# A 3x3 convolution: from a tile-scheduled, fully unrolled program to one hand-synchronised program per engine with a TensorE loop

## The chip, the cores and the metric

The kernel runs on one core of one Trainium2 chip. The metric is the time of one execution on the device in microseconds (us). The kernel before takes 125.95 us, the median of three runs (125.91 to 125.97).

## The reference

A 3x3 convolution with padding 1 and no bias: 16 images of 64 channels and 64x64 pixels, 128 output channels, all in fp32. Nine tenths of the weights are zero, at random places, and the kernel makes no use of that.

```python
x_pad = np.pad(x, ((0, 0), (0, 0), (1, 1), (1, 1)))
for b in range(16):
    for co in range(128):
        for ci in range(64):
            for kh in range(3):
                for kw in range(3):
                    output[b, co] += weight[co, ci, kh, kw] * x_pad[b, ci, kh:kh+64, kw:kw+64]
```

## The kernel before, in words

**Tiling.** Two images form a pair: 64 channels of the one on partitions 0 to 63, those of the other on 64 to 127. There are eight pairs, and each is cut into four blocks of 16 output rows, 32 blocks in all. A matmul uses 64 of the 128 rows of TensorE, so the two images of a pair go through the two halves of the array side by side; each matmul has up to 512 columns (8 rows of 64 pixels) and writes one bank of PSUM.

**Two forms of a block.** Block 0 is "direct" (`direct`, L159): for each of two groups of 8 rows, nine taps for each image, so 2 x 9 x 2 = 36 matmuls. All others use a sum shared by neighbouring rows (`twos`, L166): GpSimd adds rows pairwise into a tile `s` (L169), TensorE makes the shared product of `s` with the middle row of taps (3 taps x 2 images = 6 matmuls), ScalarE copies it from PSUM to `pc` (L176), then TensorE makes the products of the even and of the odd rows with difference weights (12 matmuls each), and VectorE adds `pc` and writes the output tile `o` (L183, four instructions a block). That is 30 matmuls a block. All matmuls stand on L150, in `product`; each is issued as a weight load and a matmul.

**Start.** SyncE (SP) loads the weights (L60) and the first 32 rows of pair 0 in fp32 (L62). GpSimd loads the rest of pair 0 (L63) and then pairs 1, 2, 3 and the first 24 rows of pair 4 (L68), converting fp32 to bf16 in the DMA. TensorE runs matmuls on zeros (`keep_busy`, L86) until the weights are there, transposes them (L111), runs seven more, and starts on block 0 when VectorE has converted the first rows (L101).

**Order.** The order of each engine's instructions is the order in which they are written; the tile framework adds the semaphores. There are eight tiles for the input, so a load never waits for a free tile. The later loads stand behind a block's GpSimd addition: the rest of pair 4 behind that of block 7, pair 5 behind block 11, pair 6 behind 15, the halves of pair 7 behind 19 and 23 (L74, L196 to L199). There are three tiles for the output, of 4 MB each. SP stores a pair when its four blocks are in the output tile (L207), and the last pair in two halves of 2 MB (L205). After the second store SP issues five loads of 4 bytes (L211), which move on which of the framework's DMA semaphores the later stores go.

Of the kernel before, what the change touches and what calls it, by code (L numbers as in the profile page):

```python
# [7 lines left out]

FP32 = mybir.dt.float32
BF16 = mybir.dt.bfloat16  # L10
ADD = mybir.AluOpType.add
SUB = mybir.AluOpType.subtract

BLOCKS = {p: "TTTT" for p in range(8)}
BLOCKS[0] = "DTTT"  # L20


G0, G1, G2, G21, G01 = range(5)
KW_ORDER = (1, 0, 2)


@with_exitstack
def kernel(
    ctx: ExitStack,
    tc: tile.TileContext,  # L30
    x: bass.AP,
    weight: bass.AP,
    out: bass.AP,
):
    nc = tc.nc

    B, C_IN, H, W = x.shape
    C_OUT, _, KH, KW = weight.shape
    assert (B, C_IN, H, W) == (16, 64, 64, 64) and (C_OUT, KH, KW) == (128, 3, 3)
    NP = B // 2  # L40
    HEAD = 32

    const_pool = ctx.enter_context(tc.tile_pool(name="const", bufs=1))
    x_pool = ctx.enter_context(tc.tile_pool(name="x", bufs=1))
    s_pool = ctx.enter_context(tc.tile_pool(name="s", bufs=3))
    p_pool = ctx.enter_context(tc.tile_pool(name="pc", bufs=4))
    o_pool = ctx.enter_context(tc.tile_pool(name="o", bufs=3))
    psum_pool = ctx.enter_context(
        tc.tile_pool(name="psum", bufs=8, space=bass.MemoryType.PSUM)
    )  # L50

    ctx.enter_context(tc.manual_schedule())


    def pair(p):
        return x[2 * p : 2 * p + 2].rearrange("n i h w -> (n i) h w")

    xs = [x_pool.tile([128, H, W], BF16, name=f"x{p}") for p in range(NP)]
    w_sb = const_pool.tile([C_OUT, C_IN * KH * KW], FP32, name="w_sb")
    nc.sync.dma_start(out=w_sb, in_=weight.rearrange("o i kh kw -> o (i kh kw)"))  # L60
    x_head = const_pool.tile([128, HEAD, W], FP32, name="x_head")
    nc.sync.dma_start(out=x_head, in_=pair(0)[:, 0:HEAD, :])  # L62
    nc.gpsimd.dma_start(out=xs[0][:, HEAD:H, :], in_=pair(0)[:, HEAD:H, :])  # L63
    ident = const_pool.tile([128, 128], BF16, name="ident")
    make_identity(nc, ident)

    def load(p, a=0, b=H):
        nc.gpsimd.dma_start(out=xs[p][:, a:b, :], in_=pair(p)[:, a:b, :])  # L68

    EARLY, CUT = 4, 24

    LATER = {2: (5,), 3: (6,), 4: (7, 0, 32), 5: (7, 32, 64)}  # L74
    for p in range(1, EARLY):
        load(p)
    load(EARLY, 0, CUT)


    idle_rhs = const_pool.tile([128, 512], BF16, name="idle_rhs")  # L80
    nc.vector.memset(idle_rhs, 0.0)  # L81
    idle_ps = psum_pool.tile([128, 512], FP32, name="ps")

    def keep_busy(n):
        for _ in range(n):
            nc.tensor.matmul(idle_ps, idle_rhs[:, 0:128], idle_rhs, start=True, stop=True)  # L86

    keep_busy(7)

    w_v = w_sb.rearrange("o (i k) -> o k i", k=KH * KW)
    w_bf = const_pool.tile([C_OUT, 3, 4 * C_IN], BF16, name="w_bf")
    w_bf4 = w_bf.rearrange("o g (k i) -> o g k i", k=4)
    wT = const_pool.tile([128, 5, 3, C_OUT], BF16, name="wT")

    def tap(g, kw, n):
        return wT[64 * n : 64 * n + 64, g, (kw - n) % 3, :]

    def cast_x(copy, a, b):  # L100
        copy(out=xs[0][:, a:b, :], in_=x_head[:, a:b, :])  # L101

    def cast(g, copy, a, b):
        k = 3 * g + a % 3
        copy(out=w_bf4[:, g, a:b, :], in_=w_v[:, k : k + b - a, :])  # L105

    def transposed(g):
        wps = psum_pool.tile([128, 4, 128], FP32, name="ps")
        for j in range(3):
            src = w_bf[:, g, C_IN * j : C_IN * (j + 2)]  # L110
            nc.tensor.matmul(wps[:, j, :], src, ident, start=True, stop=True)  # L111
        return wps[:, 0:3, :]

    def difference(g, wps):
        nc.vector.tensor_tensor(out=wT[:, g], in0=wps, in1=wT[:, G1], op=SUB)  # L115

    cast(G1, nc.vector.tensor_copy, 0, 3)
    cast(G1, nc.scalar.copy, 3, 4)
    cast(G0, nc.vector.tensor_copy, 0, 3)
    cast(G0, nc.vector.tensor_copy, 3, 4)  # L120
    cast(G2, nc.scalar.copy, 0, 3)
    cast(G2, nc.vector.tensor_copy, 3, 4)
    cast_x(nc.vector.tensor_copy, 0, 9)
    nc.scalar.copy(out=wT[:, G1], in_=transposed(G1))
    ps0 = transposed(G0)
    nc.vector.tensor_copy(out=wT[:, G0], in_=ps0)  # L126
    ps2 = transposed(G2)
    nc.scalar.copy(out=wT[:, G2], in_=ps2)
    keep_busy(7)
    cast_x(nc.scalar.copy, 9, 18)  # L130
    difference(G01, ps0)
    difference(G21, ps2)
    cast_x(nc.scalar.copy, 18, HEAD)


    def product(terms, rows):


        ps = [psum_pool.tile([128, rows, W], FP32, name="ps") for _ in range(2)]
        todo = [(t, kw) for t in terms for kw in KW_ORDER]  # L140
        for i, ((src, g, first, step), kw) in enumerate(todo):
            n_src = src.shape[1]
            lo = 0 if first >= 0 else 1
            hi = rows if first + (rows - 1) * step < n_src else rows - 1
            c_lo, c_hi = max(0, 1 - kw), min(W, W + 1 - kw)
            a = first + lo * step
            b = first + (hi - 1) * step + 1
            for n in range(2):
                q = slice(64 * n, 64 * n + 64)
                nc.tensor.matmul(  # L150
                    ps[n][:, lo:hi, c_lo:c_hi],
                    tap(g, kw, n),
                    src[q, a:b:step, c_lo + kw - 1 : c_hi + kw - 1],
                    start=(i == 0),
                    stop=(i == len(todo) - 1),
                )
        return ps

    def direct(p, o, r0, rows):  # L159
        ps = product(  # L160
            [(xs[p], G1, r0, 1), (xs[p], G0, r0 - 1, 1), (xs[p], G2, r0 + 1, 1)], rows
        )
        nc.scalar.copy(out=o[0][:, r0 : r0 + rows, :], in_=ps[0])  # L163
        nc.vector.tensor_copy(out=o[1][:, r0 : r0 + rows, :], in_=ps[1])  # L164

    def twos(p, o, r0):  # L166
        t0 = r0 // 2
        s = s_pool.tile([128, 8, W], BF16, name="s")
        nc.gpsimd.tensor_tensor(  # L169
            out=s, in0=xs[p][:, r0 : r0 + 16 : 2, :], in1=xs[p][:, r0 + 1 : r0 + 16 : 2, :], op=ADD  # L170
        )
        shared = product([(s, G1, 0, 1)], 8)
        pc = []
        for n in range(2):
            c = p_pool.tile([128, 8, W], FP32, name="pc")
            nc.scalar.copy(out=c, in_=shared[n])  # L176
            pc.append(c)
        even = [(xs[p], G21, r0 + 1, 2), (xs[p], G0, r0 - 1, 2)]
        odd = [(xs[p], G01, r0, 2), (xs[p], G2, r0 + 2, 2)]
        for first, terms in ((r0, even), (r0 + 1, odd)):  # L180
            ps = product(terms, 8)
            for n in range(2):
                nc.vector.tensor_tensor(  # L183
                    out=o[n][:, first : r0 + 16 : 2, :], in0=ps[n], in1=pc[n], op=ADD
                )

    for p in range(NP):
        both = o_pool.tile([C_OUT, 2, H, W], FP32, name="o")
        o = [both[:, n] for n in range(2)]
        into = out[2 * p : 2 * p + 2].rearrange("n o h w -> o n h w")  # L190
        last = p == NP - 1
        for blk in range(4):
            r0 = 16 * blk
            if BLOCKS[p][blk] == "T":
                twos(p, o, r0)
                if p == 1 and blk == 3:  # L196
                    load(EARLY, CUT, H)
                elif blk == 3 and p in LATER:
                    load(*LATER[p])  # L199
            else:  # L200
                for r, rows in ((r0, 8), (r0 + 8, 8)):
                    direct(p, o, r, rows)
            if last and blk % 2 == 1:
                rows = slice(r0 - 16, r0 + 16)
                nc.sync.dma_start(out=into[:, :, rows, :], in_=both[:, :, rows, :])  # L205
        if not last:
            nc.sync.dma_start(out=into, in_=both)  # L207
        if p == 1:
            spare = const_pool.tile([1, 5], FP32, name="spare")
            for k in range(5):  # L210
                nc.sync.dma_start(out=spare[:, k : k + 1], in_=weight[0:1, 0, 0, 0:1])  # L211


# [28 lines left out]
```

## Time and profile before

| what | value |
|---|---|
| median of three timed runs | 125.95 us (125.91 to 125.97) |
| span of the profiled execution | 124.3 us |
| time of a run that lies outside the span, by these two | about 1.6 us |
| TensorE busy (PE) | 108.7 us, 87% of the span, 989 matmuls |
| VectorE busy (DVE) | 82.5 us, 66% |
| ScalarE (ACT), GpSimd (POOL) | 39.0 us, 41.7 us |
| bytes written by the DMA | 42.91 MB |
| HBM read and written | 17.07 MB and 33.55 MB, 407 GB/s over the span |

The profile is of one execution, and no time was taken of that execution apart from its span. One part of the page divides the span into 40 slices and gives each engine's busy share of a slice as a digit in tenths; PEclk is the clock granted to TensorE in the same way, and DMA the busy share of the core's 16 DMA engines. Another part lists the DMA queues. A query can give the same numbers for any stretch of the span, list the instructions of a source line, and tell what each engine waited for. An `x` before a number is a count. GB/s counts bytes written at the destination; a load that converts fp32 to bf16 reads twice what it writes.

### The profile page before, as it was taken

The numbers are of one execution on the slowest core, as the hardware profiler recorded it, in microseconds if no ns is written. First come the engines' busy times: TensorE is split into PE (matmuls) and PEld (weight loads), VectorE is DVE, ScalarE is ACT, GpSimd is POOL, SyncE is SP. The second block draws the span as 40 slices with busy tenths as digits, with TensorE's granted clock in tenths as the row PEclk, the third lists the DMA queues.
The fourth block names the chain that finished last, engine by engine and source line by source line (L and its number), as shares of the span: only waits on it lengthen the run. The fifth ranks groups of instructions, "written<-read, shape, count | busy, mean of one in ns | idle before, by whom it ended". The sixth has DMA issues, their size and how long they took to land.

```text
span 124.3 us, 2453 instructions
## 1 busy us (share of the span) xinstructions
PE 108.7 (87%) x989; PEld 57.2 (46%) x989; DVE 82.5 (66%) x135; ACT 39.0 (31%) x71; POOL 41.7 (34%) x47
## 2 busy tenths in 40 slices
PE   6959999999999999999999999999999999970000
PEld 2425555555555555555555555555555555530000
DVE  0353577877787778777877878887877787772000
ACT  4543333333333333333333333333333333330000
POOL 6409333533353335333443335333333320000000
PEclk9999999999999999999999999999999999997555
DMA  4999999999999999999999999999999999999991
GB/s 120 348 220 227 219 213 213 238 411 338 335 392 422 319 316 324 377 340 329 303 385 378 354 380 443 376 349 389 418 422 437 422 427 427 437 427 403 432 414 82
DMA packets 4198, 42.91 MB, mean 345 GB/s; under 512 B 347, under 2 KB 347, under 8 KB 1115
## 3 DMA queue, kind: packets, MB, share of 16 engines
q1 hardware_dynamic: 2746, 34.90, 67.2%
q0 software_dynamic: 1440, 7.86, 30.7%
q8 instruction: 7, 0.11, 0.3%
q14 instruction: 5, 0.03, 0.1%
HBM read 17.07 MB, written 33.55 MB: 407 GB/s over the span
## 4 chain that ended last, share of the span: by engine, by line
PE 82%; DMA 5%; DVE 1%; issue 1%; DVEq 0%; SPq 0%
PE ps L150 82%; DMA x_head<-in_x_dram 5%; DVE o L183 1%; DVEq L237 0%; DVE x L101 0%; SPq L60 0%; DVEq L183 0%
## 5 line engine op out<-in xcount | busy, mean ns | idle before, releaser
L183 DVE TENSOR_TENSOR o<-ps,pc 128x512 f32<-128x512 f32 x124 | 77.8, 686 | 22.1 <-PE ps L150 19.2
L150 PE MATMUL ps<-x,wT 64*128 64x504 bf16 (+3 forms) x780 | 88.8, 373 | 1.3 <-DVE x L101 1.3
L150 PEld LDWEIGHTS <-wT 64*128 64x128 bf16 x966 | 55.2, 94 | 49.5 <-issue 1.7
L169 POOL TENSOR_TENSOR s<-x 128x512 bf16<-128x512 bf16 x31 | 35.6, 1150 | 57.6 <-PE ps L150 41.1
L176 ACT COPY pc<-ps 128x512 f32<-128x512 f32 x62 | 33.3, 589 | 64.0 <-issue 61.8
L150 PE MATMUL ps<-s,wT 64*128 64x512 bf16 (+1 forms) x186 | 25.7, 377 | 0.0
L86 PE MATMUL ps<-idle_rhs 128*128 128x512 bf16 x14 | 4.8, 505 | 1.2 <-DVE idle_rhs L81 1.2
L68 POOL DMA_DIRECT2D x<-in_x_dram x9 | 5.0, 560 | 0.0
L86 PEld LDWEIGHTS <-idle_rhs 128*128 128x128 bf16 x14 | 1.5, 118 | 3.2 <-issue 1.4
L105 DVE CAST w_bf<-w_sb 128x192 bf16<-128x192 f32 (+1 forms) x4 | 1.1, 351 | 2.5 <-DMA w_sb<-in_weight_dram 2.5
L164 DVE COPY o<-ps 128x512 f32<-128x512 f32 x2 | 1.4, 692 | 2.0 <-PE ps L150 2.0
L101 DVE CAST x<-x_head 128x576 bf16<-128x576 f32 x1 | 0.5, 460 | 2.6 <-DMA x_head<-in_x_dram 2.6
L101 ACT CAST x<-x_head 128x576 bf16<-128x576 f32 (+1 forms) x2 | 1.5, 802 | 1.8 <-DMA x_head<-in_x_dram 1.8
L163 ACT COPY o<-ps 128x512 f32<-128x512 f32 x2 | 1.2, 586 | 2.4 <-PE ps L150 2.4
L105 ACT ACT_TABLE_LOAD x1 | 1.3, 1283 | 0.7 <-PEq L226 0.7
L105 ACT CAST w_bf<-w_sb 128x64 bf16<-128x64 f32 (+1 forms) x2 | 0.7, 416 | 1.6 <-DMA w_sb<-in_weight_dram 1.6
L115 DVE TENSOR_TENSOR wT<-ps,wT 128x384 bf16<-128x384 f32 x2 | 1.0, 548 | 0.0
L111 PEld LDWEIGHTS <-w_bf 128*128 128x128 bf16 x9 | 0.5, 97 | 1.0 <-DVE w_bf L105 1.0
L63 POOL DMA_DIRECT2D x<-in_x_dram x1 | 0.7, 693 | 0.8 <-POOLq L226 0.8
L111 PE MATMUL ps<-ident,w_bf 128*128 128x128 bf16 x9 | 0.9, 222 | 0.1
L81 DVE MEMSET idle_rhs<- 128x256 uint32 x1 | 0.3, 272 | 0.9 <-PEq L226 0.9
L126 DVE CAST wT<-ps 128x384 bf16<-128x384 f32 x1 | 0.6, 551 | 0.0
(8 smaller groups left out, 1.9 us busy)
## 6 DMA issues: line engine op xcount, KB each, us to landing
out_dram<-o SPq DMA_DIRECT2D x7, 4096.0 KB, 19.8
x<-in_x_dram POOLq DMA_DIRECT2D x5, 1024.0 KB, 16.8
out_dram<-o SPq DMA_DIRECT2D x2, 2048.0 KB
x<-in_x_dram POOLq DMA_DIRECT2D x3, 512.0 KB, 13.8
x_head<-in_x_dram SPq DMA_DIRECT2D x1, 1024.0 KB, 6.2
x<-in_x_dram POOLq DMA_DIRECT2D x1, 640.0 KB, 14.8
x<-in_x_dram POOLq DMA_DIRECT2D x1, 384.0 KB, 22.3
w_sb<-in_weight_dram SPq DMA_DIRECT2D x1, 288.0 KB
```

What stands on the lines that cost most here:

```text
L68: nc.gpsimd.dma_start(out=xs[p][:, a:b, :], in_=pair(p)[:, a:b, :])
L86: nc.tensor.matmul(idle_ps, idle_rhs[:, 0:128], idle_rhs, start=True, stop=True)
L101: copy(out=xs[0][:, a:b, :], in_=x_head[:, a:b, :])
L105: copy(out=w_bf4[:, g, a:b, :], in_=w_v[:, k : k + b - a, :])
L111: nc.tensor.matmul(wps[:, j, :], src, ident, start=True, stop=True)
L115: nc.vector.tensor_tensor(out=wT[:, g], in0=wps, in1=wT[:, G1], op=SUB)
L150: nc.tensor.matmul(ps[n][:, lo:hi, c_lo:c_hi], tap(g, kw, n), src[q, a:b:step, c_lo + kw - 1 : c_hi + kw - 1], start=(i == 0), stop=(i == ...
L163: nc.scalar.copy(out=o[0][:, r0 : r0 + rows, :], in_=ps[0])
L164: nc.vector.tensor_copy(out=o[1][:, r0 : r0 + rows, :], in_=ps[1])
L169: nc.gpsimd.tensor_tensor(out=s, in0=xs[p][:, r0 : r0 + 16 : 2, :], in1=xs[p][:, r0 + 1 : r0 + 16 : 2, :], op=ADD)
L176: nc.scalar.copy(out=c, in_=shared[n])
L183: nc.vector.tensor_tensor(out=o[n][:, first : r0 + 16 : 2, :], in0=ps[n], in1=pc[n], op=ADD)
```

## The change

The kernel is written again as one program per engine inside a critical section of the framework, in which the framework adds no waits: every wait and every increment of a semaphore is written by hand.

- TensorE's program for 16 blocks (four pairs) stands once in a hardware loop that runs twice. Block 16 is the first of the second turn and so becomes direct, as block 0 is. At the end of a turn TensorE takes 16 off three semaphores. The other engines' programs stay unrolled.
- The input has four tiles (pair p in tile p mod 4) in place of eight. Loads of pairs 4 to 7 wait until TensorE has finished the blocks that read the old content: the first 24 rows of pair 4 are loaded behind GpSimd's addition of block 5 and not at the start, and wait for block 1 to be finished; the rest of pair 4 waits for block 3, pairs 5, 6 and the first half of 7 for blocks 7, 11 and 15.
- VectorE copies all four results of a direct block; before, ScalarE copied two of them.
- `s` has four tiles in place of three. TensorE waits for `e0` and `e1`, which VectorE counts up after its first and second instruction of a block, before it writes the shared and the even product of the next block.
- The five loads of 4 bytes are gone. The last four stores are waited for by hand at the end.

The core of the new file (the casts of weights and input are as before, each with its own semaphore; all of the kernel's body before goes out; abridged, `even` and `odd` stand for the lists of terms as in `twos`, and `after` adds waits to an instruction):

```python
with tc.tile_critical(no_gpsimd_drain=True):
    with nc.Block(no_gpsimd_drain=True) as block:
        @block.sync
        def _(sp):
            sp.dma_start(out=w_sb, in_=...).then_inc(S("w"), 16)
            sp.dma_start(out=x_head, in_=...).then_inc(S("xh"), 16)
            for p in range(NP - 1):
                after(sp.dma_start(out=out_of(p), in_=os[p % N_O]), ("o", 4 * p + 4)).then_inc(S(f"st{p}"), 16)
...
        @block.gpsimd
        def _(gp):
            load(0, HEAD, H)
...
            for p in range(1, SLOTS):
                load(p, 0, H)
            def free(p):
                return ("q", 16 * p - 48)
            CUT = 24
            AT = {5: [(4, 0, CUT, ("q", 8))], 7: [(4, CUT, H, free(4))], 11: [(5, 0, H, free(5))],
                  15: [(6, 0, H, free(6))], 19: [(7, 0, 32, free(7))], 23: [(7, 32, H)]}
            for b in range(NB):
                waits = [(name, 16) for name in LANDED.get(b, ())]
...
                if b - N_S >= 0 and not is_direct(b - N_S):
                    waits.append(("p", p_count(b - N_S) + 2))
                if is_direct(b):
                    after(gp.memset(mark, 0.0), *waits).then_inc(S("s"), 1)
                else:
                    after(gp.tensor_tensor(out=ss[b % N_S], in0=..., in1=..., op=ADD), *waits).then_inc(S("s"), 1)
                for l in AT.get(b, ()):
                    load(*l)
...
        @block.vector
        def _(dve):
...
            for b in range(NB):
                for k, rows in enumerate(rows_of(b)):
                    waits = [("q", 4 * b + k + 1)]
                    if b % 4 == 0 and k == 0 and p >= N_O:
                        waits.append((f"st{p - N_O}", 16))
...
                    if k != 2:
                        add.then_inc(S(("e0", "e1", None, "o")[k]), 1)
        @block.tensor
        def _(pe):
...
            with pe.Fori(0, NP // SLOTS, 1):
                for l in range(TURN):
                    xt, r0 = xs[l // 4], 16 * (l % 4)
                    free_p, free_e = ("e0", l + 1), ("e1", l + 1)
                    if is_direct(l):
...
                        continue
                    waits = [("s", l + 1), free_p]
                    product([bank(l, n) for n in range(2)], [(s, G1, 0, 1)], 8, "p", {0: waits})
                    product([bank(l, 2 + n) for n in range(2)], even, 8, "q", {0: [free_e]})
                    product([bank(l, 4 + n) for n in range(2)], odd, 8, "q", {})
                for name in ("s", "e0", "e1"):
                    pe.sem_inc(S(name), -TURN)
turn = nc.sync.to_reg(16)
for k in (5, 6, 7, 8):
    nc.sync.wait_ge(S(f"st{k}"), turn, ...)
```

Semaphore `q` counts finished output products (four a block), `p` finished shared products, `s` GpSimd's additions, `o` finished blocks in the output tile.

## The prediction on record

> **What bounds the kernel now.** I read the page's 40 slices first, then stretches between stores, then the end.
>
> ```profile
> PE   6959999999999999999999999999999999970000
> ...
> PEclk9999999999999999999999999999999999997555
> DMA  4999999999999999999999999999999999999991
> ```
>
> TensorE is full from 8 to 111 us, and the DMA engines are full from the second slice to the last but one. So two things run side by side, and the end belongs to the DMA: for 12 us after TensorE's last matmul it still works off stores. The stretches between the issues of the last full stores (87.0 and 99.8) show how little it is behind. Columns: stretch; PE, PEld, DVE, ACT, POOL busy; PEclk, DMA share, GB/s.
>
> ```profile
> core 0: us, PE busy (x) PEld busy (x) DVE busy (x) ACT busy (x) POOL busy (x), PEclk, DMA share, GB/s
> ...
> 87.00:99.80 12.80, 12.80 (x124) 6.85 (x122) 10.05 (x16) 4.29 (x9) 4.61 (x5) 1.00 1.01 429
> 99.80:124.30 24.50, 11.43 (x108) 5.88 (x104) 10.05 (x16) 3.63 (x7) 0.58 (x1) 0.78 0.89 380
> ```
>
> A pair takes 12.8 us (four blocks, 120 matmuls, 0.107 us each). After 99.8 us 380 GB/s x 24.5 us = 9.31 MB are written, but the stores issued from then on are 4.19 + 2.10 + 2.10 = 8.39 MB. So when the seventh store is issued 0.92 MB of older work is left, 2.15 us at 429 GB/s. A store's first packet comes about 1.0 us after its issue (SP issues the weight load at 0.74; the DMA share is 0.00 up to 1.7 us and 0.83 in the next). The **cover** of a late TensorE is so 1.1 us on the mean of the 16 engines. The engines do not end together, and the last one sets the time. SP's waits at the end read it:
>
> ```profile
> SPq L237 <- DMA out_dram<-o: 10.0, 3, 4.8
> ```
>
> Three waits, 10.0 us, each 2 MB half landing at most 4.8 us after what landed before it. The last landing is at about 123.45 us, so the seventh store landed near 113.75, and its 4.19 MB at 429 GB/s (9.8 us) put its predecessor's last landing at 103.95. Less 0.45 us from last packet (busy up to 123.0) to landing, the last engine was free at 103.5, against the seventh store's first packet at 100.8: 2.7 us. Cover between 1.1 and 2.7 us; I take 2.5, as the last engine decides. At other stores the backlog is larger, by the same sum 2.4 MB at 87.0 us.
>
> **The change, part by part.**
>
> *Start.* One post by SP, waited for by all, and two more branches per engine stand ahead of the first DMA. Lower bound 0.1 us (SP goes from its released wait at 0.66 to its first DMA at 0.74, a branch included); upper 0.35 us (two whole barrier rounds at the end take 0.7, from 123.6 to 124.3). Nothing is removed there, so no gain. I take **0.2**, on the path, since DMA and TensorE shift together.
>
> *End.* Four waits in a row for stores, only the last unfulfilled, an increment and a branch more, while nine of the eleven SP waits of L237 go, which stand beside the transfers. 28 ns each: between -0.1 and 0.3; I take **0.1**.
>
> *Block 16 direct.* 36 matmuls for 30: 6 x 0.107 = **0.64 us** on TensorE. VectorE copies four results of 0.69 us, 2.8 us in a block of 3.85: hidden.
>
> *Loop edge.* The body is 18 + 15 x 15 = 243 pairs of matmuls: 972 instructions with their weight loads, and some 20 waits. Instructions come by DMA:
>
> ```profile
> q8 instruction: 7, 0.11, 0.3%
> ```
>
> ```profile
> q0 software_dynamic: 41, 0.34, 107.5%
> q8 instruction: 1, 0.02, 4.1%
> ```
>
> The first is the whole span: seven packets of 16 KB. The second is 16.0 to 17.5 us, which holds the first; stretches at 31, 45 and 58 us each hold one more, 13.5 us apart, that is 13.5/0.0535 = 252 instructions. So TensorE's code streams in blocks of about 250 instructions, one at a time, and the body is four of them. The trace has no backward jump. Lower bound: nothing, if the first block is still held (never a gain: the jump only adds). Otherwise a fetch: 1.0 us to the first packet (as above), 0.98 for the packet (4.1% of 16 engines x 1.5 us), 0.45 to landing: 2.4; and with up to two 16 KB store packets ahead of it on its engine (429/16 = 27 GB/s, 0.61 us each) 3.6, which I take, since the DMA is full. Against it stands TensorE's run ahead:
>
> ```profile
> L237 PEldq DRAIN  x2: 13/1256/2498, 108.8 to 123.9; - x2
> ```
>
> The drain that follows the last matmul in the program starts at 108.8 us and waits 2.5 us; the last matmul starts at 110.9. So the sequencer is 2.1 us ahead, and can ask for the block that early. Stall 3.6 - 2.1 = **1.5 us**; ends 0 and 3.6 (no run ahead). A pause over about 2.3 us also costs clock: PEclk halves 2.3 us after the last matmul (0.90 over 111.3 to 114.0), and seven matmuls take 3.17 us cold against 1.67 warm, so add 1.5 us there. Upper end 5.1.
>
> [...]
>
> *TensorE late in all:* 0.64 + 1.5 = 2.1 us, under the cover of 2.5: nothing at the end. Without the cover it would cost 2.1. Later VectorE, stores and loads shift with TensorE.
>
> *New waits of TensorE.* `e0` needs VectorE's first instruction of the block before. It starts at 18 x 0.107 = 1.9 us of a 3.2 us block and takes 0.69: margin 0.5 us; `e1` the same. VectorE is busy 10.0 of 12.8 us and waits for TensorE, not the reverse. Taken 0; each 0.1 us missed is 3 us over 31 blocks. The extra wait instruction per block (51 ns, L150 has one at 10.2 us, with no idle of TensorE beside it) stands in the weight-load stream, which is busy 6.85 of 12.8 us: 0, ends 0 and 1.6. A gain is excluded: TensorE has no idle in mid-stream.
>
> *Ring of four.* The early load of pair 4 (0.79 MB read) moves from about 4 to 16.3 us (GpSimd reaches it after pair 1 landed near 14.0 and two additions of 1.15; block 1 is done at 15). What waits behind it is additions needed 10 us later. The start loads without it, 8.68 MB read at 412 GB/s (238 GB/s written over 1.7 to 23 us, plus the read half of the converting loads), last to 22.8 us, so it arrives in time; the rest of pair 4 then waits only for block 3, 21.7 us, against its issue at 23.5 now. Others also come 1.7 us earlier at most. Bytes are the same: 0, ends -0.5 (the DMA share is 0.97 at 21 to 24 us) and 0.5.
>
> *The five small loads* stand where SP idles until 48.6 us: 0.
>
> **Sum.** 124.3 + 0.2 + 0.1 = 124.6 us of span, and with the 1.6 us outside **126.3** (125.95 + 0.3).
>
> **Rivals.**
> 1. *The stall outruns the cover.* With the stall at 3.6 to 5.1, TensorE is 4.2 to 5.7 late; less 2.5 or 1.1 leaves 1.7 to 4.6: 128.0 to 130.9. Partly so, just past the cover, 126.7 to 128. For it: 3.6 assumes only two packets ahead. Against: 2.1 us of run ahead.
> 2. *The new waits bite* in steady state: 0.05 us a block x 31 + 2.1 = 3.7, less 2.5: 127.5. Against it: the margin of 0.5.
> 3. *Not slower.* The DMA decides, and the loads issued 1.7 us earlier close the dip at 21 to 24 us: -0.3 to -0.5 there against +0.3 at start and end: 125.6 to 126.1. It decides if TensorE stays under the cover and the DMA ends earlier than its shifted start. For it: bytes and rate are all that counts. Against it: the share is already 0.97 in the weakest stretch.
> 4. *The loop does not miss.* Then TensorE is 0.64 late, and the time is still 126.3.
>
> **Chances.** Forecast with rival 4, 126.0 to 126.7: 0.47, of which 0.30 above 126.2. Rival 1: 0.28. Rival 2: 0.07. Rival 3: 0.18, of which 0.09 below 125.7. A measurement can tell about 0.2% (0.25 us) from no change: slower 0.30 + 0.28 + 0.07 = 0.65, same 0.17 + 0.09 = 0.26, faster 0.09. Range: from 125.7 (rival 3's better half out) to 129.0 (rival 1's dearer half out, some 0.1).
>
> **What would show it.** Right: one pause of TensorE near 60 us of 1 to 2 us and none else, PEclk full; DMA share near 1 throughout, at 100 to 102 us too; the first DMA near 0.9 us. Wrong: a pause over 2.3 us with a dip in PEclk, a DMA hole after the seventh store, idle of TensorE before VectorE in every block, or a DMA hole at 22 to 25 us.

## The result, and the profile after

The changed kernel takes 127.59 us (median of four runs, 127.38 to 127.68) against 125.93 us for the kernel before beside it (125.69 to 125.97): a ratio of 1.0127, 95% interval 1.0103 to 1.0151. It is 1.3% slower, 1.3 us more than the forecast of 126.3 and inside the range. The spans are 124.34 and 125.80 us, so 1.46 of the 1.66 us stand in the trace. The rest lies outside the span (1.79 against 1.59 us). In later timed runs of the kernel before, that part is anything from 1.73 to 2.98 us, so it is given no cause.

The page of the kernel after, those rows of its 40 slices that were read of before, with the GB/s:

```profile
span 125.8 us, 2448 instructions
...
PE   5989999999999999999999999999999999970000
...
PEclk9999999999999999999999999999999999999555
DMA  3999999999999999999999999999999999999980
GB/s 90 375 225 219 219 211 211 201 159 381 429 438 294 326 313 409 391 310 300 386 401 344 359 438 387 345 380 438 427 422 438 427 432 427 425 412 425 422 372 21
```

The same row of GB/s before:

```profile
GB/s 120 348 220 227 219 213 213 238 411 338 335 392 422 319 316 324 377 340 329 303 385 378 354 380 443 376 349 389 418 422 437 422 427 427 437 427 403 432 414 82
```

The busy rows say that nothing happened: TensorE is as full as before, also in the middle where the loop jumps, its clock is full to the end, and the DMA engines are always busy. The difference is in the bytes. In the ninth slice (some 25 to 28 us) 159 GB/s stand where there were 411. "Busy" counts the time that packets are under way, and packets were slower here: the load's packets of 5 KB took up to 0.77 us (median of the half microsecond from 26.5 us), where the kernel before has 0.40 from 28 to 32 us.

The same by stretches (PE, PEld, DVE, ACT, POOL busy; PEclk, DMA share, GB/s), before and after:

```profile
21.00:24.00 3.00, 3.00 (x33) 1.68 (x30) 2.40 (x5) 1.07 (x2) 1.60 (x2) 1.00 0.97 198
24.00:27.00 3.00, 3.00 (x32) 1.57 (x30) 2.27 (x5) 1.07 (x2) 1.21 (x2) 1.00 1.09 398
27.00:30.00 3.00, 3.00 (x32) 1.58 (x30) 2.30 (x4) 1.07 (x2) 1.15 (x1) 1.00 0.96 343
```

```profile
21.00:24.00 3.00, 3.00 (x32) 1.70 (x30) 2.51 (x4) 1.07 (x2) 1.45 (x2) 1.00 1.00 203
24.00:27.00 3.00, 3.00 (x32) 1.58 (x29) 2.58 (x4) 0.96 (x2) 1.16 (x2) 1.00 1.14 171
27.00:30.00 3.00, 3.00 (x32) 1.58 (x30) 2.58 (x4) 0.83 (x3) 0.91 (x2) 1.00 0.96 267
```

Part of that is only a choice of work: a load that converts fp32 to bf16 reads twice what it writes (17.07 MB are read from HBM, for 7.86 MB written by these loads and 1.34 MB by SP's two loads). Counting the read side of these loads, at 429 GB/s, the kernel after is 0.2 us of work ahead 21 us after its first packet and some 0.87 us behind 27 us after it. So some 1.05 us is truly lost there; by 100 us some 0.4 us of that is made up again. The DMA queues in 24 to 27 us (packets, MB, share of 16 engines), before:

```profile
q1 hardware_dynamic: 64, 1.05, 83.1%
q0 software_dynamic: 63, 0.14, 25.5%
```

and after:

```profile
q0 software_dynamic: 137, 0.51, 113.9%
```

q1 carries the stores, q0 GpSimd's converting loads. Before, the first 4 MB store is issued at 23.03 us and the load of the rest of pair 4 at 23.50. After, the load comes first, at 22.53, the store at 23.55, and not one packet of the store moves until 27 us.

The end moved too. The lines of the last barrier on GpSimd and on SP (count: shortest/median/longest ns, first to last start), before:

```profile
L237 POOLq EVENT_SEMAPHORE  x4: 17/17/17, 123.6 to 124.2; - x4
...
L237 POOLq EVENT_SEMAPHORE_RANGE_CLEAR  x1: 139/139/139, 123.9 to 123.9; - x1
```

and after:

```profile
L365 POOLq EVENT_SEMAPHORE  x4: 17/17/17, 124.5 to 125.7; - x4
...
L365 SPq EVENT_SEMAPHORE  x2: 17/17/17, 125.0 to 125.7; - x2
...
L365 POOLq EVENT_SEMAPHORE_RANGE_CLEAR  x1: 244/244/244, 125.3 to 125.3; - x1
```

GpSimd's first post is at 124.5 us and SP's at 125.0; from GpSimd's first barrier instruction to its next the trace has 0.45 us, where the kernel before has 0.08. The instruction that clears the semaphores takes 244 ns in place of 139.

**Three terms of the span.** First DMA packet: 1.76 us before, 1.98 after, +0.22. From the first to the last packet: 121.24 and 121.91, **+0.67**. From the last packet to the end of the span: 1.35 and 1.91, **+0.56**. Together 1.45. TensorE itself is later by 1.2 us at the last store, which costs nothing, as shown below.

### The profile page after: what moved, and what is told of

Its sections match the earlier page's. It is cut to its first block, busy times and chain, and to the rows that moved or that the text cites. A ratio compares the mean times of both kernels' runs of the same rounds, so it can differ in the third digit from the quotient of the medians.

```text
span 125.8 us, 2448 instructions
## 1 busy us (share of the span) xinstructions
PE 110.5 (88%) x995; PEld 58.1 (46%) x995; DVE 85.3 (68%) x137; ACT 36.7 (29%) x67; POOL 41.0 (33%) x48
## 3 DMA queue, kind: packets, MB, share of 16 engines
q0 software_dynamic: 1440, 7.86, 31.3%
HBM read 17.07 MB, written 33.55 MB: 402 GB/s over the span
## 4 chain that ended last, share of the span: by engine, by line
PE 82%; DMA 5%; DVE 1%; issue 1%; DVEq 0%; SPq 0%
PE ps L290 82%; DMA x_head<-in_x_dram 5%; DVE o L244 1%; DVEq L119 0%; DVE x L98 0%; SPq L123 0%; SPq L365 0%; SPq L118 0%
## 5 line engine op out<-in xcount | busy, mean ns | idle before, releaser
L290 PE MATMUL ps<-x,wT 64*128 64x504 bf16 (+3 forms) x792 | 89.9, 374 | 0.5 <-DVE x L98 0.5
L244 DVE TENSOR_TENSOR o<-ps,pc 128x512 f32<-128x512 f32 x120 | 76.8, 686 | 19.4 <-PE ps L290 19.2
L290 PEld LDWEIGHTS ps<-x,wT 64*128 64x128 bf16 x792 | 45.2, 94 | 40.1 <-issue 1.0
L214 ACT COPY pc<-ps 128x512 f32<-128x512 f32 x60 | 32.2, 589 | 69.4 <-PE ps L290 69.4
L190 POOL TENSOR_TENSOR s<-x 128x512 bf16<-128x512 bf16 x30 | 34.5, 1153 | 49.8 <-PE ps L290 43.4
L290 PE MATMUL ps<-s,wT 64*128 64x512 bf16 (+1 forms) x180 | 24.9, 377 | 0.0
L290 PEld LDWEIGHTS ps<-s,wT 64*128 64x128 bf16 x180 | 10.3, 94 | 8.8
L240 DVE COPY o<-ps 128x512 f32<-128x512 f32 x8 | 5.2, 686 | 2.5 <-PE ps L290 2.5
L257 PEld LDWEIGHTS ps<-idle_rhs 128*128 128x128 bf16 x14 | 1.8, 137 | 3.9 <-issue 2.4
L206 ACT CAST wT<-ps 128x384 bf16<-128x384 f32 x1 | 0.5, 478 | 0.4 <-PE ps L262 0.4
L205 ACT CAST wT<-ps 128x384 bf16<-128x384 f32 x1 | 0.5, 478 | 0.4 <-PE ps L262 0.4
```

What stands on the lines that cost most here:

```text
L190: gp.tensor_tensor(out=ss[b % N_S], in0=xt[:, r0 : r0 + 16 : 2, :], in1=xt[:, r0 + 1 : r0 + 16 : 2, :], op=ADD,),
L205: after(act.copy(out=wT[:, G1], in_=wps(G1)), ("t", 1)).then_inc(S("a"), 1)
L214: act.copy(out=pcs[(2 * b + n) % N_PC], in_=bank(b, n)),
L240: add = dve.tensor_copy(out=rows, in_=bank(b, (0, 1, 4, 5)[k]))
L244: add = dve.tensor_tensor(out=rows, in0=bank(b, 2 + k), in1=pcs[(2 * b + k % 2) % N_PC], op=ADD)
L257: mm = pe.matmul(idle_ps, idle_rhs[:, 0:128], idle_rhs, start=True, stop=True)
```

## The experiments

Two theories stood against each other. By the theory of order, the load that is issued ahead of the first store costs the DMA about 0.7 us, and the rest of the change little. By the theory of lateness, the hole is a by-product (the ring of four, the loop, later data), and the parts of the change cost what they cost. A theory of parts holds that start and end explain what the DMA does not.

What the runs gave, in one table; "rest" is the span less the DMA's stretch, that is start and end together (the spans of the experiments are known to 0.1 us):

| kernel | rest of pair 4 / first store issued at | DMA, first to last packet | GB/s, 24 to 27 us | span | rest | ratio to before, interval |
|---|---|---|---|---|---|---|
| before | 23.50 / 23.03 | 121.24 | 398 | 124.3 | 3.1 | 1 |
| after | 22.53 / 23.55 | 121.91 | 171 | 125.8 | 3.9 | 1.0127 (1.0103 to 1.0151) |
| loop undone | 22.73 / 23.75 | 121.95 | 157 | 125.8 | 3.9 | 1.0105 (1.0039 to 1.0171) |
| loop and ring undone | 19.90 / 22.55 | 122.08 | 140 | 126.0 | 3.9 | 1.0111 (1.0045 to 1.0177) |
| after, one load behind the store | 23.31 / 22.74 | 121.24 | 382 | 125.1 | 3.9 | see below |
| synchronisation by hand alone | 23.46 / 22.95 | 120.99 | 376 | 124.4 | 3.4 | 1.0002 (0.9968 to 1.0036) |
| after, loads behind stores, padded | 23.16 / 22.59 | 121.26 | 388 | 124.6 | 3.3 | 1.0005 (0.9979 to 1.0031) |
| before, load ahead of the store | 20.15 / 22.86 | 121.99 | 145 | 125.1 | 3.1 | 1.0067 (1.0037 to 1.0097) |

**1. The loop alone undone.** The same hand-written programs, TensorE's body written out 32 times.

```diff
-with pe.Fori(0, NP // SLOTS, 1):
-    for l in range(TURN):
-        xt, r0 = xs[l // 4], 16 * (l % 4)
+if True:
+    for l in range(NB):
+        xt, r0 = xs[l // 4 % SLOTS], 16 * (l % 4)
...
-    for name in ("s", "e0", "e1"):
-        pe.sem_inc(S(name), -TURN)
```

> Only the hardware loop is undone: TensorE's 32 blocks stand one after the other, block 16 stays direct, four input tiles stay. Theory A (the loop edge is free, the time lies in the DMA between 23 and 29 us and at the two ends of the program): span and time as of the changed kernel, 125.8 us and 127.6 us within 0.3; seven or eight code packets in place of four. Theory B (the loop costs, by the edge or by holding the code): 0.5 us or more faster than the changed kernel.

Span (125.8 us) and time (127.57 us, median of four) are those of the kernel after. The loop is worth nothing, and no jump's cost was being hidden in the 1.3%.

**2. Loop and ring undone.** Eight input tiles, the first 24 rows of pair 4 loaded at the start, later loads without waits; the four sum tiles stay.

```diff
 (as in run 1, and)
-SLOTS = 4
-TURN = 4 * SLOTS
+SLOTS = NP
+TURN = 16
...
+load(4, 0, CUT)
-AT = {5: [(4, 0, CUT, ("q", 8))], 7: [(4, CUT, H, free(4))], ...
+AT = {7: [(4, CUT, H)], 11: [(5, 0, H)], 15: [(6, 0, H)], ...
```

> The loop and the ring of four are undone: eight input tiles, the first 24 rows of pair 4 loaded at the start, no load waits for TensorE. GpSimd still has four sum tiles, so the rest of pair 4 is issued at about 21 us, ahead of the first store. Theory of order (a load that is issued just ahead of the first store holds the store's packets back by 4 us and does not fill the engines alone): the hole between 23 and 29 us stays, 1 us, time near 127.5. Theory of lateness (the hole comes because the DMA queues run nearly empty when pair 4's early part comes late): the hole goes, time near 126.6.

The hole stays:

```profile
24.00:27.00 3.00, 3.00 (x30) 1.56 (x28) 2.34 (x5) 1.07 (x2) 1.16 (x1) 1.00 0.99 140
```

So it is not the ring. Without the wait for a free tile the load goes out at 19.90 us, more than three microseconds earlier than before, because with four sum tiles GpSimd runs one block further ahead. The edit of run 4 differs from this one in the number of sum tiles and in block 16, and there the load is back at 23.46 us; block 16 comes long after. By this pair of runs the fourth sum tile turned the order round; in the kernel after, the wait for block 3 only held the load back to 22.53. A ring of four with three sum tiles was not run.

**3. The kernel after, with that one load behind the addition of block 8.** GpSimd then issues it just after the first store.

```diff
-7: [(4, CUT, H, free(4))],
+8: [(4, CUT, H, free(4))],
```

> The changed kernel with one edit: the rest of pair 4 is loaded behind GpSimd's addition of block 8 in place of block 7, at about 24.3 us, so just after the first store (23.55). Theory of order: the first store's packets start about 1.3 us after its issue as before the change, the hole of 1.1 us goes, span near 124.8 and time near 126.6. Theory of lateness: the hole stays or grows, since the queues are still nearly empty at 24 us; time 127.6 or more.

Queues in 24 to 27 us:

```profile
q1 hardware_dynamic: 61, 1.00, 78.1%
q0 software_dynamic: 64, 0.15, 27.0%
```

The store flows as before, and the DMA's stretch is 121.24 us, that of the kernel before to the hundredth. The span falls by 0.7 us. Its four times scatter from 126.89 to 131.44 us (ratio 1.0128, 1.004 to 1.0217), so they decide nothing. The trace, which is of the fastest of the four, shows the hole gone in that execution; run 7 has the times. The second store still has its load ahead here (34.53 against 35.55 us), and by the count with the read side some 0.3 us goes there, between 37 and 39 us.

**4. Synchronisation by hand alone.** Written out, eight tiles, loads as before, three sum tiles, block 16 not direct.

```diff
 (as in run 2, and)
-N_S = 4
+N_S = 3
...
-return b % TURN == 0
+return b == 0
```

> The hand-written synchronisation alone: TensorE unrolled, eight input tiles, loads issued where the kernel before issues them, three sum tiles, only block 0 direct. Theory of parts: no hole between 23 and 29 us, first packets 0.2 us later than before, the end 0.2 to 0.6 us longer (0.37 of it only if GpSimd's code lies as in the changed kernel): span 124.8 to 125.2, time 126.3 to 126.8. If hand synchronisation costs in mid-stream too, span 125.5 or more.

The hand-written form with its critical section costs nothing that can be measured in the time: 126.17 us (median of ten), a ratio of 1.0002, with the order back and no gap at GpSimd's barrier. That is less than was expected (span 124.4 against 124.8 to 125.2): the first packet is 0.22 us later as in the kernel after, but the end grows by 0.04 us only, and the DMA's stretch came out 0.24 us shorter than before in the one execution that was profiled.

**5. Sixteen small instructions more in GpSimd's program.** Queue q14 carries code too, in packets of 8 KB. In the kernel after, one such packet starts at 125.9 us, about 1 us after the gap of 0.45 us at GpSimd's barrier. Runs 1, 2 and 3 have the same gap and a packet 0.7 to 1 us after it; run 4, whose GpSimd program is two instructions longer, has its last packet at 117.9 and no gap. One-column memsets of a scratch tile, after the first loads, move GpSimd's later code.

```diff
+pad = pool.tile([128, 16], FP32, name="pad")
...
+for k in range(16):
+    gp.memset(pad[:, k : k + 1], 0.0)
```

> The changed kernel with 16 one-column memsets more in GpSimd's program, at about 4.5 us where it idles; they compute nothing that is used. GpSimd spends 0.45 us between taking and releasing the last-but-one barrier, where it spent 0.08 before the change. If that comes from where its code lies in the blocks in which code is loaded, the gap moves or goes (span 0.4 shorter); if it belongs to the critical section's end, it stays at 0.45 and the span stays at 125.8.

With them, and with no other program changed, a packet comes at 68 us, none comes at the end, and the gap is 0.08. So the gap goes with where GpSimd's code lies; since the packet starts only after the gap, the gap is not a wait for that packet's data, and what fills it stays open. In the execution that was profiled the first rows landed at 10.45 us, 2.5 late, so its span (128.8) is not compared with the others. The median of eleven runs is 127.4 us, a ratio of 1.009 (1.006 to 1.0121): by the ratios some 0.4 us less than the kernel after, the size of the gap, though the two intervals overlap and the medians are only 0.2 us apart.

This late execution also parts the order from the moment of the load. Its load goes out at 25.03 us, later than in any kernel without the hole, but ahead of its store at 26.05. The hole is there, and the store's first packet comes 5.1 us after its issue:

```profile
27.00:30.00 3.00, 3.00 (x31) 1.60 (x28) 2.33 (x5) 1.07 (x2) 1.16 (x1) 1.00 0.91 116
```

**6. A body that can't be held.** 66 matmuls of two columns on zeros ahead of each shared product make the body about 2,950 instructions, some 190 KB by the 16 KB for about 250 instructions of the kernel before. Only the backward jump is read: whether TensorE still passes it without a pause when the body is three times as long. The matmuls do work that the reference does not have, and are overwritten; the one time that was taken, 191.02 us, is not read.

```diff
+for i in range(66):
+    mm = pe.matmul(bank(l, 0)[:, 0, 0:2], idle_rhs[:, 0:128], idle_rhs[:, 0:2], start=True, stop=True)
+    if i == 0:
+        after(mm, *waits)
```

> The changed kernel with 66 two-column matmuls on zeros ahead of each shared product (they write a bank that the product then overwrites), so that the loop body has about 2950 instructions, 190 KB, in place of about 1000, 64 KB. [...] The time itself is longer by the added matmuls, some 60 to 200 us.

The loop's branch in the kernel after:

```profile
L302 PEldq COMPARE_BRANCH  x2: 76/152/229, 58.8 to 110.6; - x2
```

and with the long body:

```profile
L302 PEldq COMPARE_BRANCH  x2: 79/1800/3521, 86.5 to 179.0; - x2
```

Of the two, the one that jumps back is the longer. TensorE around it with the long body (start, duration, group, idle before it):

```profile
85.72 2.68 PE L290 MATMUL ps<-x,wT 64*128 64x512 bf16 x24
90.31 2.04 PE L290 MATMUL ps<-x,wT 64*128 64x512 bf16 x18 [1.92 <-issue]
```

And TensorE's code packets (q8) of the whole span, after and with the long body:

```profile
q8 instruction: 4, 0.07, 0.2%
```

```profile
q8 instruction: 24, 0.39, 0.8%
```

The packets from the jump at 58.76 us to the end, in the kernel after and in the unrolled run 1:

```profile
q8 instruction: 1, 0.02, 0.1%
```

```profile
q8 instruction: 5, 0.08, 0.4%
```

The kernel after moves four packets, its body about once. The one behind the jump starts at 60.57 us, when TensorE's sequencer has already run the first instruction of the second turn (L311, at 59.04); run 1 has a packet at the same place (60.86). None follows in the other 50 us of the turn, so the second turn runs from code that is held. The long body moves 11 packets before its jump and 13 after it, its branch takes 3.52 us and TensorE pauses 1.92.

**7. The kernel after, each load from the second part of pair 4 on one block later, with the sixteen memsets.** The loop and the ring of four stay.

```diff
 (as in run 5, and)
-7: [(4, CUT, H, free(4))], 11: [(5, 0, H, free(5))], 15: [...], 19: [...], 23: [...]
+8: [(4, CUT, H, free(4))], 12: [(5, 0, H, free(5))], 16: [...], 20: [...], 24: [...]
```

> The changed kernel with each load from pair 4's second part on issued one block later, so just after a store and not just ahead of one, and with the 16 memsets that moved GpSimd's code. Theory of order: no hole at 23 to 29 us, none at 36 to 42 us either, end 0.37 us shorter: span 124.3 to 124.8, time 126.0 to 126.5, so within 0.5 us of the kernel before. Rival (the ring's waits or the loop cost otherwise): span stays above 125.3.

```profile
24.00:27.00 3.00, 3.00 (x30) 1.60 (x28) 2.33 (x5) 1.07 (x2) 1.15 (x1) 1.00 1.10 388
```

```profile
L368 POOLq EVENT_SEMAPHORE  x4: 17/17/17, 123.8 to 124.5; - x4
...
L368 SPq EVENT_SEMAPHORE  x2: 17/17/17, 123.9 to 124.5; - x2
```

Both losses are gone: 388 GB/s in the hole's place, and SP follows GpSimd's post after 0.1 us where it was 0.5. The median of twelve runs is 126.20 us, a ratio of 1.0005 (0.9979 to 1.0031). Run 5, which differs from this one in the places of the loads alone, has 1.009 (1.006 to 1.0121), so what the order of the loads is worth shows in the times as well. This is the best form with the loop that was found; it can't be told from the kernel before and does not beat it.

**8. The kernel before, with the order turned round.** One number: the rest of pair 4 behind the addition of block 6 in place of block 7.

```diff
-if p == 1 and blk == 3:
+if p == 1 and blk == 2:
```

> The kernel before with one edit: the rest of pair 4 is loaded behind block 6 of GpSimd in place of block 7, at about 20.4 us, ahead of the first store (23.0) and not behind it. Theory of order: the first store's packets start 4 us after its issue, the DMA loses about 1 us between 23 and 29 us, span near 125.3, time near 126.9. If order does not matter in itself: span 124.3, time 125.9.

```profile
24.00:27.00 3.00, 3.00 (x31) 1.57 (x29) 2.27 (x5) 1.07 (x2) 1.16 (x1) 1.00 1.07 145
```

```profile
q0 software_dynamic: 118, 0.43, 107.2%
```

The hole appears in a kernel that has nothing else of the change. The DMA's stretch grows by 0.75 us, the span by 0.8, the time by 0.67%. With runs 3, 5 and 7 this settles the order as the cause of the DMA's loss: putting it right takes the loss away, putting it wrong brings it.

## Why the prediction was right in sign and low in size

The sign was right, but most of the change came through steps that the forecast had at or near nothing, and run 7, without them, is not slower than the kernel before. That the time lies inside the range is luck: the part of the range above 126.7 us stood for rivals 1 and 2, and neither happened.

- **Start, 0.2.** Right: the first packet is 0.22 us later, SP's first load starts at 0.95 us.
- **Block 16, 0.64 us on TensorE.** Right: TensorE's chain (start, duration, group) is 102.74 us where it was 102.09, before and after:

```profile
7.95 102.09 PE ps L150 x954
```

```profile
8.58 102.74 PE ps L290 x960
```

- **Loop edge, a stall of 1.5 us (rival 4: none).** Wrong, and rival 4 held. The step that failed is "So TensorE's code streams in blocks of about 250 instructions, one at a time", taken to mean that the first block is gone after 972 instructions. Microsecond by microsecond around the jump at 58.8 us TensorE is full:

```profile
57.00:58.00 1.00, 1.00 (x14) 0.51 (x10) 0.99 (x2) 0.00 (x0) 0.00 (x0) 1.00 0.97 328
58.00:59.00 1.00, 1.00 (x12) 0.52 (x10) 0.78 (x2) 0.86 (x2) 0.78 (x1) 1.00 1.05 328
59.00:60.00 1.00, 1.00 (x12) 0.57 (x10) 0.56 (x1) 0.21 (x1) 0.38 (x1) 1.00 1.05 319
```

  The packets in the trace of before showed when code arrives, not when it is dropped. A body of 64 KB is held, one of 190 KB is not. Where it does miss (run 6), the fetch took 3.5 us, the run ahead some 1.5 and the pause 1.9, near the 3.6, 2.1 and 1.5 of the forecast, but not by its sum: the DMA engines were only 0.13 to 0.27 busy then, so no two packets stood in the way. The code packet started 0.96 us after the branch and took 1.07; from its end to the end of the branch 1.49 us passed, where the forecast had 0.45. In the kernel after, the branch back over four packets of code took 0.23 us, and no packet came before its target ran. No size between 64 and 190 KB was run, so from which size on a body is no longer held is not shown.
- **Cover of 2.5 us.** Right as far as it was tried: the seventh store is issued at 101.04 us (99.81 before, +1.23), and the DMA engines have no hole behind it. They were themselves some 0.6 us late then, so only about 0.6 us of the cover was drawn on:

```profile
99.00:102.00 3.00, 3.00 (x32) 1.68 (x30) 2.42 (x5) 1.07 (x2) 0.00 (x0) 1.00 1.00 426
102.00:105.00 3.00, 3.00 (x31) 1.61 (x28) 2.34 (x5) 1.07 (x2) 0.00 (x0) 1.00 1.00 426
```

- **New waits of TensorE, 0.** Right: TensorE waits for nothing in mid-stream, and VectorE still waits for TensorE:

```profile
DVE o L244 <- PE ps L290: 19.2, 30, 0.7
```

- **Ring of four, "0, ends -0.5 ... and 0.5".** The step that failed. The forecast saw that "the rest of pair 4 then waits only for block 3, 21.7 us, against its issue at 23.5 now", and reckoned "Bytes are the same". It did not ask what the load is moved past: SP's queue, with the first store at 23.03 us. It measured +0.67 us, outside the bounds. By runs 2 and 4 it hangs not on the ring but on the fourth sum tile that went with it, for which the forecast has no term. The last sentence of the forecast did name "a DMA hole at 22 to 25 us" as a sign of being wrong; it came between 24 and 28. Rival 3 counted on the same earlier loads for a gain and had their sign wrong.
- **End, 0.1 (ends -0.1 and 0.3).** Mis-sized: 0.56 us, outside its bounds. From the last packet to its landing 0.45 us pass in both kernels; it is the closing barrier that grew. Of that, 0.42 go with the sixteen memsets (the gap, 0.37 more than before, and 0.05 in the drain behind it); they belong to the length of GpSimd's program and to no part of the change as such. The rest stays in run 7 too, most of it in the clearing of the semaphores (244 ns against 139).
- **Rivals 1 and 2** did not happen, though rival 2 (127.5) and rival 1 (with what it calls "just past the cover", 126.7 to 128) give the time that came. The number alone would have confirmed a wrong cause.

The sum, with what was measured: 0.22 + 0.67 + 0.56 = 1.45 of span, where the forecast had 0.3.

## What to carry to other kernels

When an edit moves a transfer, list what it is moved past on the other queues as well, and compare issue times to the fraction of a microsecond: here the same bytes took the DMA 0.67 us longer at equal "busy" (171 GB/s at a share of 1.14 in 24 to 27 us, 398 at 1.09 before), and GB/s with the read side counted showed it. A loop over a body is judged by whether its code is still held, which the run with a longer body showed at once (a branch back of 0.23 us with 64 KB, of 3.52 with some 190). When a span grows at its end, look for a code packet near the gap (here about 1 us behind a gap of 0.45), and move the code with a few idle instructions, before blaming the change.

## What the runs showed of the hardware

**Which of a converting load and the first store went first was worth 0.75 us of the DMA's stretch (run 8).** With the load first, its packets of 5 KB, which take 0.40 us once both queues flow, take 0.41 to 0.77 in the kernel after between 24.5 and 28.5 us (medians of half microseconds), the loads fall to 118 to 156 GB/s from some 200, and the store's first packet comes 4.4 to 4.6 us after its issue (kernel after, runs 1, 2 and 8). With the store first, its first packet comes after 1.3 us (kernel before) to 1.8 us, the load's first packet 4.8 to 5.4 us after its issue, and nothing is lost. Once both flow, as many packets of the one move as of the other: 16 of 16 KB and 16 of 5 KB in each microsecond from 29 to 31 us of the kernel before. The second comer waited over 4 us in either order (a load in part behind older loads of its own queue), and it cost throughput in one order alone. Where inside the DMA engines the lost microsecond goes was not tried and stays open. Later loads that came just ahead of a store lost less: 0.3 us at the second store of run 3, nothing that shows at the load issued at 60.95 us in the kernel after, where older stores were still moving (60 packets of q1 in 60 to 63 us, 380 GB/s).

**The slowest DMA engine ended the kernel.** In run 7 the DMA engines are by the mean of bytes moved some 0.4 us ahead of the kernel before, counted from the first packet, and the DMA's stretch is the same. By their packets the 16 engines end some 2 us apart (121.0 to 123.0 us before), and the mean's gain does not reach the last one.
